# A hybrid SSD and attention layer: first pair's k copied by two engines, last product's matmuls pinned and cut, its stores on two queues

## The chip, the core and the metric

The kernel runs on one core of one Trainium2 chip. The metric is the device time of one execution in microseconds (us); the figure to be predicted is the median over repeated executions. Before the change it is 835.93 us, the median of three runs (835.86, 835.93 and 838.29).

The core's engines are TensorE (PE, with its weight loads as PEld), VectorE (DVE), ScalarE (ACT), GpSimd (POOL) and SyncE (SP), which here only issues DMAs.

## What is computed

One decoder layer over 512 tokens of width 1024. One projection of the normalised input feeds an SSD head group and a forgetting-attention head group of 16 heads of 64; then come an output projection, and a gated MLP of width 2816 with a short convolution. Cut to the two places that the change touches:

```python
qh = rms_norm(heads(q), q_norm_w)
kh = rms_norm(heads(k), k_norm_w)
for start in range(0, s, Q_BLOCK):                       # 128 queries at a time
    end = start + Q_BLOCK
    logits = einsum('bhqd,bhkd->bhqk', qh[:, :, start:end], kh[:, :, :end]) * scale
    logits = logits + cum[:, :, start:end, None] - cum[:, :, None, :end]
    p = softmax(where(causal, logits, -inf))
    outs.append(einsum('bhqk,bhkd->bhqd', p, vh[:, :, :end]))
...
h = causal_depthwise_conv(x @ w_up, conv_w, conv_b)
gate, val = split(h, 2, axis=-1)
x = x + (silu(gate) * val) @ w_down                      # 512 x 2816 times 2816 x 1024
```

## The kernel before

**Precision.** A float32 operand is split into a high part in float32r and a low part (the rest). `mm3` (L108 to L112) makes one product as three matmuls: high by high (L110), high by low (L111), low by high (L112). Weights are split as they arrive, by `load_split` (L99): SP loads `wraw`, ACT casts it to `wh` (L104), and DVE or POOL subtracts to make `wl` (L105).

**Order.** The program is recorded in source order, and a scheduler that models the engines then places the instructions of each engine's queue. `urgent()` (L594) raises the priority of what is recorded inside it, so attention work is slotted between projection matmuls. A changed dependency can therefore move many instructions in a stretch, not only the edited ones. Each queue executes in the order that it was given.

**Attention.** Heads are taken in pairs. `fox_qk` (L489) transposes a pair's normalised k and q into one PSUM bank each (`qkT`, L496). For k it writes head by head the high part (ACT, L503) and the low part (DVE, L504), each on that head's own 64 partitions, and then SP copies high and low together to the other 64 partitions with a DMA within SBUF (L506, 256 KB a head, 16 of them in the program). For q the high part goes to the own half and the low part to the other half. With k in both halves, one matmul over 128 partitions adds q high and q low. `fox_probs` (L510) then makes, for each of four query blocks, the scores `S` with two matmuls (k high L539, k low L540), the row maximum on DVE (L541), the exponential on ACT (L545), and after all four the reciprocal (L546) and the scaling (L549) on DVE. The biases `bias` (L524 to L529) are made ahead on ACT, DVE and POOL. `fox_values` (L552) transposes the probabilities (L566), splits them (L568, L569) and multiplies by v (L580).

While heads run, the projections of the next group of four heads serve as filler on PE: `token_block` (L318) with its matmuls into `pq`. After a block of q or k, ACT copies and squares it (L460, L462), DVE reduces (L463), POOL takes the power -1/2 (L122), and DVE scales `tok` (L468), which the next transposes (L496) need. v takes one ACT (L478) and one DVE instruction (L479) for each block.

**Last product.** The down projection is made of seven products of half size (`PRODUCTS`, L822). A product takes 11 blocks of 128 rows of its weight, in units of two (the last unit has one), for two token blocks `i`, each into its own PSUM bank. In the seventh (`Y`, lhs S3) the matmuls of the last two units are held and recorded together: 3 blocks x 2 token blocks x 3 matmuls = 18 matmuls of 512 columns, sorted by `i` (L865), though the scheduler is free to place them. When a bank is complete, DVE adds it to `x2` at column 0 and subtracts it at column 512 (L881), and SP stores the finished rows (L883); for `i` = 1 both are cut into halves of 256 columns. That makes six adds and six stores at the end of the program, all stores on SP's queue.

Of the kernel before, what the change touches and what calls it, by code (L numbers as in the profile page):

```python
# [10 lines left out]
AF = mybir.ActivationFunctionType  # L11
ALU = mybir.AluOpType
# [3 lines left out]
P = 128  # L16
# [39 lines left out]
def tile_hybrid_layer(  # L56
# [19 lines left out]
    nc = tc.nc  # L76
    act, dve, pool, pe = nc.scalar, nc.vector, nc.gpsimd, nc.tensor
# [10 lines left out]
    def raw(ap):  # L88
        return ap.bitcast(F32)
# [15 lines left out]
        (sub or dve).tensor_tensor(out=l, in0=r, in1=raw(h), op=ALU.subtract)  # L105
        return h, l

    def mm3(o, ah, al, bh, bl, start, stop, grouped=True):  # L108
        kw = {} if grouped else {"skip_group_check": True}
        pe.matmul(o, ah, bh, start=start, stop=False, **kw)  # L110
        pe.matmul(o, ah, bl, start=False, stop=False, **kw)  # L111
        pe.matmul(o, al, bh, start=False, stop=stop, **kw)  # L112

    def bank(name="g"):
        return pg.tile([P, 512], F32, tag="g", name=name)
# [373 lines left out]
    def fox_qk(pair, tq, tk):  # L489
        qs = [pf.tile([P, SEQ], F32R, tag="qs", name="qs", bufs=4) for _ in range(2)]  # L490
        ks = [pf.tile([P, 2, SEQ], F32R, tag="ks", name="ks", bufs=4) for _ in range(2)]
        pr = pair % 2
        for tok, w in ((tk, kw), (tq, qw8)):
            t = mbank("qkT")
            for tb in range(NTB):
                pe.transpose(t[:, tb * P : (tb + 1) * P], tok[:, tb, pr * P : (pr + 1) * P], ident)  # L496
            for hd, (own, other) in enumerate(HALVES):
                src, sw = t[own, :], w[own]
                if tok is tq:
                    h, l = qs[hd][own, :], qs[hd][other, :]  # L500
                else:
                    h, l = ks[hd][own, 0, :], ks[hd][own, 1, :]
                act.activation(h, src, AF.Copy, scale=sw)  # L503
                dve.scalar_tensor_tensor(out=l, in0=src, scalar=sw, in1=raw(h), op0=ALU.mult, op1=ALU.subtract)  # L504
                if tok is tk:
                    nc.sync.dma_start(raw(ks[hd][other, :, :]), raw(ks[hd][own, :, :]))  # L506
        osum = pf.tile([P, SEQ], F32, tag="osum", name="osum", bufs=2)
        return qs, ks, osum
# [334 lines left out]
    for n, (quarter, _, tiles, start, adds) in enumerate(PRODUCTS):  # L843
# [7 lines left out]
        for u, (lo, hi) in enumerate(UNITS):  # L851
# [9 lines left out]
                continue  # L861
            todo = [(k, i, b) for b in held for k in range(b[0], b[1]) for i in range(2)]
            held = []
            if final and u == len(UNITS) - 1:
                todo.sort(key=lambda t: t[1])  # L865
            for k, i, (lo_, _, h_, l_) in todo:
                c = slice((k - lo_) * 512, (k - lo_ + 1) * 512)
                s = slice(i * P, (i + 1) * P)
                mm3(
                    tiles[i], lhs[0][:, k, s], lhs[1][:, k, s], h_[:, c], l_[:, c], start and k == 0, k == NH - 1,  # L870
                    grouped=False,
                )
                if k == NH - 1:
                    for row, col, op, done in adds:
                        tb = row + i
                        cuts = 2 if final and i == 1 else 1
                        w = 512 // cuts
                        for cut in range(cuts):
                            c = slice(cut * w, (cut + 1) * w)
                            oc = slice(col + cut * w, col + (cut + 1) * w)  # L880
                            dve.tensor_tensor(out=x2[:, tb, oc], in0=x2[:, tb, oc], in1=tiles[i][:, c], op=op)  # L881
                            if done:
                                nc.sync.dma_start(out[tb * P : (tb + 1) * P, oc], x2[:, tb, oc])  # L883


def _feature(w, np):
# [74 lines left out]
```

## Time and profile before

| | |
|---|---|
| median of 3 runs | 835.93 us (835.86 to 838.29) |
| the profiled execution | 839.82 us, its span 838.0 us |
| busy share of the span | PE 97%, PEld 84%, DVE 75%, ACT 52%, POOL 35% |
| granted TensorE clock, mean | 0.995 |
| DMA | 98.76 MB, mean 118 GB/s |

The span runs from the first to the last instruction of the profiled execution; 1.8 us of its time lie outside. All positions below are microseconds from the start of that span. A busy PE in these tables includes the modelled end of pipelined matmuls, so the distance between the starts of two matmuls, not the duration shown, is what one costs in a stream.

### The profile page before, as it was taken

The page shows a single profiled execution, that of the slowest core. Times are in us where ns is not written, and L with a number is a line of the kernel's source. Part 1 is how long each engine was busy: PE and PEld are TensorE (multiplying, and loading weights), DVE is VectorE, ACT ScalarE, POOL GpSimd, SP SyncE. Part 2 cuts the span into 40 slices and gives each one's busy share as a digit, 9 for nine tenths or more (in the row PEclk, how much of TensorE's full clock was granted, in tenths as well). Part 3 has the DMA queues.
Part 4 walks back from the last instruction along what each step waited for, and adds up shares of the span by engine and source line. Part 5 has one row for each costly group of instructions (what it writes and reads, how often), then busy time and mean ns, then how long its engine had stood idle before and what let it go on. Part 6 is the DMA issues. An engine that isn't in the chain of part 4 may idle for free.

```text
span 838.0 us, 12428 instructions
## 1 busy us (share of the span) xinstructions
PE 810.0 (97%) x4590; PEld 700.4 (84%) x4590; DVE 630.9 (75%) x1015; ACT 435.9 (52%) x845; POOL 290.5 (35%) x281
## 2 busy tenths in 40 slices
PE   8999989899979999899999999999999999999997
PEld 5788879779979899799898898888888888888885
DVE  7596898775759798898999667666666666887744
ACT  5346645434456687576566255444433444656531
POOL 4125253365535445125233423333333332133120
PEclk9999999999989999999999999999999999999999
DMA  8424332341333333243422244233233223399992
GB/s 315 158 83 131 101 94 85 104 136 51 113 102 106 100 100 112 84 120 101 126 72 66 90 121 134 100 98 101 101 101 99 82 96 101 115 253 182 208 190 84
DMA packets 31565, 98.76 MB, mean 118 GB/s; under 512 B 4048, under 2 KB 5136, under 8 KB 31504
## 3 DMA queue, kind: packets, MB, share of 16 engines
q1 hardware_dynamic: 28048, 86.43, 31.9%
q0 software_dynamic: 3456, 11.54, 7.6%
q8 instruction: 36, 0.59, 0.3%
q14 instruction: 25, 0.20, 0.1%
HBM read 91.56 MB, written 2.20 MB: 112 GB/s over the span
## 4 chain that ended last, share of the span: by engine, by line
PE 73%; DVE 11%; issue 6%; POOL 3%; ACT 3%; DMA 2%; SPq 0%; DVEq 0%; POOLq 0%; ACTq 0%
PE up L112 10%; PE up L111 9%; PE up L110 9%; PE pq L111 4%; PE pq L112 4%; PE pq L110 4%; PE po L112 3%; PE po L111 3%; PE po L110 3%; DVE xs L351 2%; PE Y L110 2%; PE Y L112 2%; PE Y L111 2%; PE o L580 2%; PE pT L566 1%
## 5 line engine op out<-in xcount | busy, mean ns | idle before, releaser
L104 ACT CAST wh<-wraw 128x1024 fp32r<-128x1024 f32 x103 | 108.5, 1053 | 137.6 <-PE up L111 72.1
L110 PE MATMUL pq<-wh,xh 128*128 128x256 f32 x512 | 146.7, 289 | 0.0
L112 PE MATMUL pq<-wh,xl 128*128 128x256 f32 x512 | 146.7, 287 | 0.0
L111 PE MATMUL pq<-wl,xh 128*128 128x256 f32 x512 | 145.6, 285 | 0.5 <-DVE wl L105 0.5
L112 PE MATMUL up<-hh,wl 128*128 128x512 f32 (+1 forms) x368 | 140.2, 381 | 0.2 <-DVE wl L105 0.2
L111 PE MATMUL up<-hl,wh 128*128 128x512 f32 (+1 forms) x368 | 139.9, 380 | 0.0
L110 PE MATMUL up<-hh,wh 128*128 128x512 f32 (+1 forms) x368 | 139.8, 380 | 0.0
L105 POOL TENSOR_TENSOR wl<-wraw,wh 128x1024 fp32r<-128x1024 f32 x31 | 75.1, 2424 | 108.9 <-ACT wh L104 99.9
L105 DVE TENSOR_TENSOR wl<-wraw,wh 128x1024 fp32r<-128x1024 f32 x72 | 89.5, 1243 | 20.0 <-ACT wh L104 19.9
L111 PEld LDWEIGHTS pq<-wl,xh 128*128 128x128 f32 x512 | 98.2, 192 | 1.9 <-DVE wl L105 0.9
L110 PEld LDWEIGHTS pq<-wh,xh 128*128 128x128 f32 x512 | 98.0, 192 | 1.9 <-issue 1.2
L112 PEld LDWEIGHTS pq<-wh,xl 128*128 128x128 f32 x512 | 98.2, 192 | 0.7 <-issue 0.5
L112 PEld LDWEIGHTS up<-hh,wl 128*128 128x128 f32 x368 | 69.2, 188 | 13.5 <-DVE wl L105 0.4
L110 PEld LDWEIGHTS up<-hh,wh 128*128 128x128 f32 x368 | 69.1, 188 | 13.3 <-issue 0.2
L111 PEld LDWEIGHTS up<-hl,wh 128*128 128x128 f32 x368 | 69.2, 188 | 13.2
L773 DVE TENSOR_TENSOR up<-up,R 128x512 f32<-128x512 f32 x44 | 30.3, 691 | 57.0 <-PE up L112 57.0
L778 DVE SCALAR_TENSOR_TENSOR ua<-up,pc,ua 128x511 f32<-128x511 f32 (+1 forms) x88 | 67.2, 766 | 3.2 <-ACT ua L776 1.7
L526 POOL TENSOR_SCALAR bias<-cum,tokS 128x256 f32<-128x256 f32 (+1 forms) x32 | 22.5, 711 | 91.2 <-DVE nm L541 91.2
L545 ACT ACTIVATE prob<-prob,nm 128x128 f32<-128x128 f32 (+1 forms) x64 | 35.9, 562 | 29.6 <-DVE nm L541 29.3
L254 DVE TENSOR_TENSOR x<-po,x 128x512 f32<-128x512 f32 x64 | 43.3, 684 | 10.1 <-PE po L112 9.5
L734 ACT CAST wh<-T 128x1024 fp32r<-128x1024 f32 (+1 forms) x30 | 29.3, 978 | 37.5 <-PE Z L112 15.6
L735 DVE TENSOR_TENSOR wl<-T,wh 128x1024 fp32r<-128x1024 f32 (+1 forms) x30 | 33.8, 1133 | 19.7 <-ACT wh L734 19.7
(237 smaller groups left out, 1862.9 us busy)
## 6 DMA issues: line engine op xcount, KB each, us to landing
wraw<-in_wup_dram SPq DMA_DIRECT2D x44, 512.0 KB, 3.3
wraw<-in_wqkv_dram SPq DMA_DIRECT2D x24, 512.0 KB, 3.3
T<-in_wdown_dram POOLq DMA_DIRECT2D x20, 512.0 KB, 7.8
wraw<-in_wout_dram SPq DMA_DIRECT2D x16, 512.0 KB, 3.3
wraw<-in_wxbc_dram SPq DMA_DIRECT2D x11, 512.0 KB, 4.6
T<-in_wdown_dram SPq DMA_DIRECT2D x10, 512.0 KB, 5.1
wraw<-in_wdown_dram SPq DMA_DIRECT2D x10, 512.0 KB, 3.7
wraw<-in_wz_dram SPq DMA_DIRECT2D x8, 512.0 KB, 3.3
```

What stands on the lines that cost most here:

```text
L104: act.copy(h, r)
L105: (sub or dve).tensor_tensor(out=l, in0=r, in1=raw(h), op=ALU.subtract)
L110: pe.matmul(o, ah, bh, start=start, stop=False, **kw)
L111: pe.matmul(o, ah, bl, start=False, stop=False, **kw)
L112: pe.matmul(o, al, bh, start=False, stop=stop, **kw)
L254: dve.tensor_add(dst, o, dst)
L526: (dve if qb == 2 else pool).tensor_scalar(out=b, in0=cum[:, :n], scalar1=-1.0, scalar2=edge, op0=ALU.mult, op1=ALU.add)
L545: act.activation(p, p, AF.Exp, scale=-1.0, bias=nm[:, qb : qb + 1], accum_out=sm[:, qb : qb + 1])
L734: act.copy(h[:, :n], src[:, :n])
L735: dve.tensor_tensor(out=l[:, :n], in0=src[:, :n], in1=raw(h[:, :n]), op=ALU.subtract)
L773: dve.tensor_mul(xp, o, R2)
L778: dve.scalar_tensor_tensor(out=a[:, s:], in0=xp[:, : SEQ - s], scalar=pc[:, cw + 2 - s : cw + 3 - s], in1=a[:, s:], op0=ALU.mult, op1=ALU.add,
```

## The change

- In `fox_qk`, for the first pair of heads alone, the copy of k into the other 64 partitions is no longer a DMA. ACT writes the high part a second time from the same PSUM bank, and DVE the low part: two ACT and two DVE instructions of 64x512 more, two DMAs of 256 KB less. The other seven pairs keep the DMA.
- In the last two units of the last product, the matmuls keep the order of the program (`keep_in_program_order`): first the nine of token block 0 with 512 columns, then nine on columns 0 to 255 of token block 1, then nine on columns 256 to 511: 27 matmuls where there were 18.
- The adds are recorded behind them, token block 0 first, then the halves of token block 1. Of the six final stores, the three of columns from 512 on go to ACT's queue, the others stay with SP.

The diff, with the parts left out that only rename:

```diff
-    def mm3(o, ah, al, bh, bl, start, stop, grouped=True):
+    def mm3(o, ah, al, bh, bl, start, stop, grouped=True, keep=False):
         kw = {} if grouped else {"skip_group_check": True}
-        pe.matmul(o, ah, bh, start=start, stop=False, **kw)
-        pe.matmul(o, ah, bl, start=False, stop=False, **kw)
-        pe.matmul(o, al, bh, start=False, stop=stop, **kw)
+        for n, (a, b) in enumerate(((ah, bh), (ah, bl), (al, bh))):
+            ins = pe.matmul(o, a, b, start=start and n == 0, stop=stop and n == 2, **kw)
+            if keep:
+                tc.keep_in_program_order(ins)
...
                 dve.scalar_tensor_tensor(out=l, in0=src, scalar=sw, in1=raw(h), op0=ALU.mult, op1=ALU.subtract)
-                if tok is tk:
+                if tok is tk and pair == 0:
+                    act.activation(ks[hd][other, 0, :], src, AF.Copy, scale=sw)
+                    dve.scalar_tensor_tensor(
+                        out=ks[hd][other, 1, :], in0=src, scalar=sw, in1=raw(h), op0=ALU.mult, op1=ALU.subtract
+                    )
+                elif tok is tk:
                     nc.sync.dma_start(raw(ks[hd][other, :, :]), raw(ks[hd][own, :, :]))
...
+            def add_out(i, part_):
+                for row, col, op, done in adds:
+                    tb = row + i
+                    oc = slice(col + part_.start, col + part_.stop)
+                    dve.tensor_tensor(out=x2[:, tb, oc], in0=x2[:, tb, oc], in1=tiles[i][:, part_], op=op)
+                    if done:
+                        (nc.scalar if final and col else nc.sync).dma_start(
+                            out[tb * P : (tb + 1) * P, oc], x2[:, tb, oc]
+                        )
...
             if final and u == len(UNITS) - 1:
-                todo.sort(key=lambda t: t[1])
+                halves = (slice(0, 256), slice(256, 512))
+                for k, i, blk in todo:
+                    if i == 0:
+                        product(k, i, blk, whole, keep=True)
+                for half in halves:
+                    for k, i, blk in todo:
+                        if i == 1:
+                            product(k, i, blk, half, keep=True)
+                add_out(0, whole)
+                for half in halves:
+                    add_out(1, half)
+                continue
```

`product` calls `mm3` for one block of weight rows and the given columns of the bank.

The scheduler's order changes in two stretches alone: around the first heads of attention, and at the end.

**PE at the first head.** The names are `S` for scores (L539, L540, in the change L545, L546: k high, k low) and `pq` for projection filler (`mm3`, in the change all on L111). Before:

```order
L112 MATMUL pq<-wh,xl 128x256
L539 MATMUL S<-ks,qs 128x128
L540 MATMUL S<-ks,qs 128x128
L539 MATMUL S<-ks,qs 128x256
L540 MATMUL S<-ks,qs 128x256
L539 MATMUL S<-ks,qs 128x384
L540 MATMUL S<-ks,qs 128x384
L539 MATMUL S<-ks,qs 128x512
L540 MATMUL S<-ks,qs 128x512
L110 MATMUL pq<-wh,xh 128x256 x2
```

Now:

```order
L545 MATMUL S<-ks,qs 128x128
L545 MATMUL S<-ks,qs 128x256
L111 MATMUL pq<-wh,xl 128x256
L111 MATMUL pq<-wh,xh 128x256
L111 MATMUL pq<-wl,xh 128x256
L111 MATMUL pq<-wh,xl 128x256
L546 MATMUL S<-ks,qs 128x128
L546 MATMUL S<-ks,qs 128x256
L545 MATMUL S<-ks,qs 128x384
L546 MATMUL S<-ks,qs 128x384
L111 MATMUL pq<-wh,xh 128x256 x2
L111 MATMUL pq<-wl,xh 128x256
```

The first scores stand four filler matmuls earlier, they are no longer in one run, and the scores of the last query block (128x512) follow 23 filler matmuls behind those of the third.

**DVE at the same place.** `ks`, `qs` and `v` are the low parts of k, q and v; `prob,nm` is the row maximum of a score block. Before:

```order
L504 SCALAR_TENSOR_TENSOR ks<-qkT,pc,ks 64x512
L504 SCALAR_TENSOR_TENSOR qs<-qkT,qw_221,qs 64x512
L479 SCALAR_TENSOR_TENSOR v<-pq,r,v 128x2x64
L504 SCALAR_TENSOR_TENSOR ks<-qkT,pc,ks 64x512
L504 SCALAR_TENSOR_TENSOR qs<-qkT,qw_221,qs 64x512
L479 SCALAR_TENSOR_TENSOR v<-pq,r,v 128x2x64 x3
L541 ISA prob,nm<-S,bias 128x128
```

Now:

```order
L505 SCALAR_TENSOR_TENSOR ks<-qkT,pc,ks 64x512
L505 SCALAR_TENSOR_TENSOR qs<-qkT,qw_221,qs 64x512
L480 SCALAR_TENSOR_TENSOR v<-pq,r,v 128x2x64
L508 SCALAR_TENSOR_TENSOR ks<-qkT,pc,ks 64x512
L505 SCALAR_TENSOR_TENSOR qs<-qkT,qw_221,qs 64x512
L480 SCALAR_TENSOR_TENSOR v<-pq,r,v 128x2x64 x2
L505 SCALAR_TENSOR_TENSOR ks<-qkT,pc,ks 64x512
L547 ISA prob,nm<-S,bias 128x128
```

The second copy of the first head's k takes the place that the second head's k had; the second head's k follows two v instructions later, and its own second copy (L508) stands behind the first head's third score block. On ACT the same happens with L507.

**PE at the end.** `Y` are the two banks of the last product; `oh`, `ol` the high and low part of S3. The last rows before:

```order
L110 MATMUL Y<-wh,oh 128x512 x2
L111 MATMUL Y<-wl,oh 128x512
L112 MATMUL Y<-wh,ol 128x512
L110 MATMUL Y<-wh,oh 128x512
L111 MATMUL Y<-wl,oh 128x512
L112 MATMUL Y<-wh,ol 128x512
L111 MATMUL Y<-wl,oh 128x512
L112 MATMUL Y<-wh,ol 128x512
```

Now (the three rows of 128x512 come three times in a row, those of 128x256 six times, for three blocks and two halves):

```order
L111 MATMUL Y<-wh,oh 128x512
L111 MATMUL Y<-wl,oh 128x512
L111 MATMUL Y<-wh,ol 128x512
L111 MATMUL Y<-wh,oh 128x256
L111 MATMUL Y<-wl,oh 128x256
L111 MATMUL Y<-wh,ol 128x256
```

Before, the two banks were interleaved block by block to the end; now bank 0 is complete 18 half-width matmuls before the end, and the first half of bank 1 nine before it.

## Rows read from the trace of the kernel before

**Rows 1.** The page, its first part: busy time, share of the span, instructions.

```profile
PE 810.0 (97%) x4590; PEld 700.4 (84%) x4590; DVE 630.9 (75%) x1015; ACT 435.9 (52%) x845; POOL 290.5 (35%) x281
```

**Rows 2.** Windows: stretch, length, each engine's busy time, granted clock, DMA share, GB/s.

```profile
236.00:246.00 10.00, 5.88 (x27) 5.72 (x28) 3.11 (x12) 3.01 (x10) 3.13 (x7) 0.66 0.23 70
246.00:256.00 10.00, 10.00 (x83) 9.87 (x83) 8.49 (x21) 8.46 (x20) 5.06 (x7) 1.00 0.31 108
...
239.00:240.00 1.00, 0.00 (x0) 0.00 (x0) 0.00 (x0) 0.00 (x0) 0.00 (x0) 0.50 0.67 262
...
700.00:800.00 100.00, 100.00 (x440) 82.22 (x439) 76.45 (x94) 55.69 (x80) 25.25 (x26) 1.00 0.73 181
```

**Rows 3.** PE's waits from 225 to 300: in total, times, longest.

```profile
PE S L539 <- DMA ks<-ks: 4.5, 1, 4.5
PE qkT L496 <- DVE tok L468: 1.2, 1, 1.2
```

**Rows 4.** PE's timeline: start, duration, instruction, [idle before and its releaser].

```profile
231.11 0.28 PE L110 MATMUL pq<-wh,xh 128*128 128x256 f32 x1
231.23 0.28 PE L111 MATMUL pq<-wl,xh 128*128 128x256 f32 x1
...
235.31 0.28 PE L112 MATMUL pq<-wh,xl 128*128 128x256 f32 x1
240.12 0.45 PE L539 MATMUL S<-ks,qs 128*128 128x128 f32 x1 [4.53 <-DMA ks<-ks]
...
243.46 0.41 PE L110 MATMUL pq<-wh,xh 128*128 128x256 f32 x1
243.67 0.41 PE L111 MATMUL pq<-wl,xh 128*128 128x256 f32 x1
...
245.38 0.31 PE L110 MATMUL pq<-wh,xh 128*128 128x256 f32 x1
```

**Rows 5.** All 16 copies of k by DMA (L506): issue to landing.

```profile
DMA to landing us min/median/max: 2.8/2.9/8.3
```

**Rows 6.** ACT's and DVE's timelines from 231 to 251.

```profile
231.70 0.68 ACT L503 ACTIVATE ks<-qkT,pc 64x512 fp32r<-64x512 f32 x1
...
232.82 0.76 DVE L504 SCALAR_TENSOR_TENSOR ks<-qkT,pc,ks 64x512 fp32r<-64x512 f32 x1
...
240.94 0.29 DVE L541 CUSTOM_DVE_ANT_0 prob<-S,bias 128x128 f32<-128x128 f32 x1 [5.41 <-PE S L540]
...
241.81 0.42 DVE L541 CUSTOM_DVE_ANT_0 prob<-S,bias 128x256 f32<-128x256 f32 x1 [0.58 <-PE S L540]
...
246.13 0.29 DVE L541 CUSTOM_DVE_ANT_0 prob<-S,bias 128x128 f32<-128x128 f32 x1 [1.42 <-PE S L540]
...
250.75 0.18 DVE L546 RECIPROCAL sm<-sm 128x4 f32<-128x4 f32 x1 [1.24 <-ACT prob L545]
```

**Rows 7.** DVE's timeline: the two scalings of group 1's `tok`.

```profile
264.00 1.23 DVE L468 TENSOR_TENSOR tok<-tok,ms 128x1024 f32<-128x1024 f32 x1 [1.32 <-POOL ms L122]
...
282.63 3.42 DVE L468 TENSOR_TENSOR tok<-tok,ms 128x1024 f32<-128x1024 f32 x1 [2.80 <-POOL ms L122]
```

**Rows 8.** Timeline of the end, PE, DVE and SP.

```profile
831.58 0.39 PE L111 MATMUL Y<-wl,oh 128*128 128x512 f32 x1
...
831.78 2.61 DVE L881 TENSOR_TENSOR x<-x,Y 128x512 f32<-128x512 f32 x6 [5.08 <-PE Y L112]
831.81 0.40 PE L112 MATMUL Y<-wh,ol 128*128 128x512 f32 x1
...
833.98 0.41 DVE L881 TENSOR_TENSOR x<-x,Y 128x256 f32<-128x256 f32 x1
...
835.02 0.40 SPq L883 DMA_DIRECT2D out_dram<-x  x1
```

**Rows 9.** DMA issues: the last store of 835.02, and POOL's loads from 790 on.

```profile
out_dram<-x SPq DMA_DIRECT2D x1, 128.0 KB, 2.0
...
T<-in_wdown_dram POOLq DMA_DIRECT2D x5, 512.0 KB, 6.5
```

More of the change, by code (lines that the diff above doesn't have):

```diff
@@ L863, in tile_hybrid_layer, with product @@
             held = []
-            if final and u == len(UNITS) - 1:
-                todo.sort(key=lambda t: t[1])
[L866 to L872, printed above, removed]
-                if k == NH - 1:
[L874 to L883, printed above, removed]
+            def product(k, i, b, part_, keep=False):
+                lo_, _, h_, l_ = b
+                s = slice(i * P, (i + 1) * P)
+                c = slice((k - lo_) * 512 + part_.start, (k - lo_) * 512 + part_.stop)
+                mm3(
+                    tiles[i][:, part_], lhs[0][:, k, s], lhs[1][:, k, s], h_[:, c], l_[:, c], start and k == 0,
+                    k == NH - 1, grouped=False, keep=keep,
+                )
@@ new lines, in add_out @@
+            def add_out(i, part_):
[6 more added lines that the diff above has]
+                            out[tb * P : (tb + 1) * P, oc], x2[:, tb, oc]
+                        )
@@ new lines, in tile_hybrid_layer @@
+            whole = slice(0, 512)
+            if final and u == len(UNITS) - 1:
+                halves = (slice(0, 256), slice(256, 512))
[10 more added lines that the diff above has]
+                continue
@@ L886, in _feature @@
+            for k, i, blk in todo:
+                product(k, i, blk, whole)
+                if k == NH - 1:
+                    add_out(i, whole)
 def _feature(w, np):
```

## The prediction

> **What bounds the kernel now.** I read the page first: PE is busy for 97% of the span, DVE for 75%, the others for less [rows 1]. So time is won where PE stands still or runs slowly, or after its last matmul, and nowhere else. The windows then show where it stands still: from 236 to 246 PE is busy for 5.88 of 10 us and its granted clock averages 0.66, and in that stretch DVE, ACT and POOL are each busy for only about 3 [rows 2]. In the next ten PE is full at clock 1.00, and so it is in a hundred microseconds near the end (700 to 800) [rows 2]; what is won at 240 is therefore not soaked up by slack that late. The waits name the cause: the scores of the first head wait 4.5 us for the copy of k by DMA. From 225 to 300 the only other wait of PE over 1 us is one of 1.2 for `tok` [rows 3].
>
> PE's timeline shows what the wait costs behind it. The last filler starts at 235.31; the next matmul starts at 240.12, after 4.53 idle [rows 4]. By 239 the granted clock stood at 0.50, that is at 1.2 instead of 2.4 GHz [rows 2]. Filler matmuls that were 0.12 apart before the gap (231.11, 231.23) are 0.21 apart behind it (243.46, 243.67), until about 245.38 [rows 4]. The copy is an odd one: the median of all 16 copies lands 2.9 us after its issue, the slowest 8.3 [rows 5].
>
> The end of the program is the other place. The last matmul starts at 831.81 and takes 0.40, so PE ends at 832.21. DVE had waited 5.08 for a complete bank, and all six adds run from 831.78 on, the last from 833.98 to 834.39. SP's last store is issued at 835.02, 0.63 behind the add that it carries away [rows 8], and lands 2.0 later, at 837.02 [rows 9]; the span ends at 838.0.
>
> **The change at the first head.** Removed: two DMAs of 256 KB and the wait. The scores now need the second copy of the first head's k. It takes the place in ACT's and DVE's order that the second head's k had: ACT from 231.70 for 0.68, DVE from 232.82 for 0.76 [rows 6], so both parts lie there by 233.6. PE reaches the scores, now four fillers earlier, at 235.31 - 3 x 0.12 = 234.95 [rows 4]. The wait goes entirely.
>
> What that is worth for PE: 4.53 of idle time, and the slow stretch. From 240.12 to 245.38 are 5.26 us; at 0.12 for 0.21 this work takes 3.0 (2.26 less), at half the clock exactly 2.63 less. I take 2.4, since this stretch holds both filler and scores. Upper end for PE: 4.53 + 2.4 = 6.9.
>
> Added: one ACT and one DVE instruction for each of two heads, 2 x 0.68 and 2 x 0.76 [rows 6]. They lie in the time in which both engines now wait for the first scores. DVE is the tighter of the two, and it decides how much of PE's lead lasts, because the probabilities go through it. Up to the second head's reciprocal it idles 5.41 + 0.58 + 1.42 + 1.24 = 8.65 us [rows 6]. If all of this went and 1.5 of new work came, DVE would be 7.1 ahead, more than PE. If the last two waits stay (the second head's scores and ACT's exponential still follow each other in the new order), it is 7.1 - 1.42 - 1.24 = 4.5 ahead. So this part is worth between 4.5 and 6.9. I take **6.0**, nearer the upper end: in the new order 23 fillers stand between the third and fourth score blocks, so PE has other work while DVE catches up. If that cover were gone, PE would wait for DVE and the 4.5 would hold. Next in line is the second head's second copy, queued on DVE behind three row maxima of the first head, and then the 1.2 for `tok`, which I leave as it is.
>
> On SP the two copies leave the queue, and the loads behind them move up. I cost this at nothing: no wait for a weight load shows beside the copy [rows 3].
>
> **The change at the end.** PE: nine 512-wide matmuls 0.23 apart (831.58, 831.81) become eighteen 256-wide ones at 0.12 (the filler's width and distance) [rows 4, 8]: 2.07 becomes 2.16, 0.1 more, so PE ends at 832.3. In exchange bank 0 is complete 18 x 0.12 = 2.2 before the end and the first half of bank 1 is complete 1.1 before it. Four of the six adds fit beside these matmuls, for the six take 2.61 in all [rows 8]. Behind the last matmul only two 256-wide adds remain, at most 2 x 0.41 = 0.8 [rows 8], to 833.1. The store of the second goes to ACT's queue, on which only two earlier ones stand, and nothing follows. Issued at 833.1 instead of 835.02, it ends the program **1.9** earlier. What waits on SP now (a store every half microsecond behind its add) is split in two.
>
> The trace has no DMA issued by ACT. The nearest row, same tile and size from SP, lands in 2.0; the dearest other queue, POOL's loads of 512 KB, takes 6.5 [rows 9]. At 6.5 the end would come at 839.6 instead of 837.0, 2.6 later than now. I take 2.0, for it is the same store, and keep the other end for the range.
>
> **Sum.** 6.0 + 1.9 = 7.9. The profiled execution took 839.82 us, so it would take 831.9. It lies 3.9 above the median of the runs, 835.93. I carry the whole sum over: **828.0 us**.
>
> **Rival 1: the timed runs stall less than the profiled one.** The slow copy may be the profiled execution's own: other copies land in 2.9 [rows 5], and the execution is 3.9 longer than the median. If all 3.9 were this stall, the median becomes 831.9. If only the clock part were missing, the sum is 6.0 - 2.4 + 1.9 = 5.5, hence 830.4; the three runs, 838.29 against 835.9 twice, differ by about these 2.4. Against it: a profile lengthens other things too, and the copy stands behind the same loads in every run.
>
> The Trainium skill ("TensorE: Matmul & The Clock Gate", section "What's actually happening") says that the clock's change comes at a different point of the work from run to run; by that rule some runs of this kernel stall without the slow stretch, the 830.4 above. One trace cannot show it.
>
> **Rival 2: the lead is lost again.** PE waits for `tok` and its fellows anyway, and those chains of ACT, DVE and POOL may come no earlier. Then only the end is won: 834.0. For it speaks DVE at 8.49 of 10 us behind the stall [rows 2]; against it, that these chains begin with matmuls that come earlier.
>
> **Rival 3, slower: the lead becomes one new gap.** Its place is group 1's `tok`, which the transposes of the third pair need. If POOL's power and DVE's scaling come no earlier than now, PE stands there with its whole lead, 6.9 + 1.2 us, the clock falls as it did by 239, and the slow stretch costs 2.4 again: 835.93 + 2.4 - 1.9 = 836.4. If the first `tok` then also takes 3.42 instead of 1.23, as the second does [rows 7], it is 838.6. It decides as soon as `tok` gains less than about 3 us. For it: DVE waits for POOL there, 1.32 and 2.80 [rows 7].
>
> **Rival 4: ACT's stores are dear.** At POOL's 6.5 the end loses 4.5 against my sum: 832.5.
>
> **Numbers.** Forecast 48%, rival 1 28%, rival 2 11%, rival 3 7%, rival 4 6%. A measurement of this kernel tells 0.3%, 2.5 us, from no change: faster is below 833.4, slower above 838.4. Faster takes in the forecast and rivals 1 and 4: 82%. Rival 2 and half of rival 3 fall within: 14%. Slower: 4%. The range begins at 826.0: 6.9 + 1.9, and the wait of 1.2 for `tok` gone as well, are 10.0 less. It ends at 832.6, with rivals 1 and 4; rivals 2 and 3, 18%, lie outside.
>
> **What would show it.** In the new profile no wait of PE for `ks` at the first head; PE full and at clock 1.00 from 236 to 246; the first score about 235 instead of 240.1; the filler behind it 0.12 apart. At the end: four adds before the last matmul, two behind it; ACT's last store issued 0.8 behind PE's end, landing in about 2. Wrong would be a new gap of PE before 300, above all at a transpose for `tok` or a score block behind DVE; a landing of ACT's store far above 2; or a median that falls by 2 to 4 although the profile shows all of this, which is rival 1.

## The result, and the profile after

The changed kernel takes 828.99 us, the median of four runs (828.33 to 830.26), beside 836.89 for the kernel before on the same chip (835.86 to 838.29): a ratio of 0.9906, 95% interval 0.9884 to 0.9929. That is 7.9 us less. Its profiled execution took 829.39 us with a span of 827.6; the spans of the two profiled executions differ by 10.4, more than the medians do. That gap between 7.9 and 10.4 has to be explained too. One execution of head_only (its profiled one) and one of before_low_dve (both kernels are described below) took 2062 and 1620 us and stand in no median below, so head_only has no profile to read.

The page's first part, and the windows of the changed kernel (as [rows 1, 2]):

```profile
PE 807.4 (98%) x4599; PEld 698.7 (84%) x4599; DVE 629.7 (76%) x1017; ACT 437.2 (53%) x847; POOL 293.8 (36%) x281
```

```profile
236.00:246.00 10.00, 10.00 (x83) 9.82 (x81) 8.78 (x28) 8.02 (x24) 5.88 (x8) 1.00 0.33 97
246.00:256.00 10.00, 10.00 (x84) 9.91 (x83) 9.71 (x23) 7.81 (x17) 5.61 (x7) 1.00 0.48 131
276.00:286.00 10.00, 10.00 (x84) 9.91 (x84) 7.44 (x18) 7.95 (x19) 2.83 (x2) 1.00 0.46 117
...
326.00:336.00 10.00, 7.50 (x55) 6.53 (x54) 7.14 (x10) 4.75 (x11) 3.70 (x2) 1.00 0.18 60
```

From 236 to 246 PE is busy for all of 10.00 us where it was for 5.88, and the granted clock is 1.00 instead of 0.66. What is left stands later: 2.5 us are missing from 326 to 336.

PE's timeline at the first head (as [rows 4]):

```profile
234.80 0.39 PE L545 MATMUL S<-ks,qs 128*128 128x128 f32 x2
235.03 0.28 PE L111 MATMUL pq<-wh,xl 128*128 128x256 f32 x1
...
235.50 0.40 PE L546 MATMUL S<-ks,qs 128*128 128x128 f32 x2
...
236.32 0.28 PE L111 MATMUL pq<-wl,xh 128*128 128x256 f32 x1
236.44 0.28 PE L111 MATMUL pq<-wh,xl 128*128 128x256 f32 x1
```

The first score starts at 234.80 instead of 240.12, without a wait, and the filler behind it goes at 0.12.

PE's waits from 225 to 350, before (more of the view of [rows 3], which ended at 300):

```profile
PE S L539 <- DMA ks<-ks: 4.9, 2, 4.5
PE qkT L496 <- DVE tok L468: 2.5, 2, 1.3
PE po L110 <- DVE v L479: 1.2, 1, 1.2
PE pT L566 <- DVE nm L541: 0.6, 1, 0.6
PE pq L111 <- DVE wl L105: 0.5, 1, 0.5
```

and in the changed kernel, from 225 to 345:

```profile
PE qkT L497 <- DVE tok L469: 1.3, 1, 1.3
PE po L111 <- DVE v L480: 1.2, 1, 1.2
PE pT L572 <- DVE nm L547: 0.7, 1, 0.7
```

`po` is the output projection's product and `pT` the transposed probabilities. The waits for `ks` are gone. So are two that the change doesn't touch: 1.17 for group 1's second `tok`, and 0.46 for a `wl` ahead of it. Three of before's remain, all of group 2: 1.3 for `tok`, 1.2 for `v` and 0.7 for `nm`.

The end, on DVE, SP and ACT (as [rows 8]):

```profile
820.80 1.28 DVE L884 TENSOR_TENSOR x<-x,Y 128x512 f32<-128x512 f32 x2 [3.49 <-PE Y L111]
822.93 1.41 DVE L884 TENSOR_TENSOR x<-x,Y 128x256 f32<-128x256 f32 x4 [0.86 <-PE Y L111]
...
821.51 2.86 SPq L886 DMA_DIRECT2D out_dram<-x  x3
...
L886 ACTq DMA_DIRECT2D out_dram<-x x3: 338/339/383, 822.1 to 824.4; - x3
...
DMA to landing us min/median/max: 1.8/2.0/2.1
```

PE's last matmul starts at 822.62 and ends at 822.90. The last row is the landing of these six stores. Only two adds stand beside matmuls. All four of token block 1 start behind the very last one, the two of the first half too, whose columns were complete 1.1 us before. ACT's last store is issued 1.5 us behind PE's end; before, SP's last was 2.8 behind it.

**One way to divide the span.** The transposes of k and q (`qkT`) begin the attention and end with the last pair, so their first and last start cut the span in three: what lies ahead, the attention, and the rest with the MLP and the end. In this table the last column but one sums the gaps between one matmul's end and the next one's start, inside the middle stretch, from PE's timeline.

| profiled execution | first `qkT` | first to last | PE idle in it | last `qkT` to the end |
|---|---|---|---|---|
| before | 229.5 | 199.9 | 9.7 | 408.7 |
| before_again (below) | 228.8 | 198.3 | 8.7 | 408.6 |
| changed | 229.4 | 190.6 | 3.3 | 407.6 |
| tail_only | 228.1 | 196.0 | 8.0 | 407.5 |
| head_act_queue | 229.5 | 191.5 | 3.2 | 407.4 |
| head_double | 228.6 | 187.6 | 0.8 | 407.6 |
| all_pairs | 230.4 | 188.2 | 0.5 | 407.6 |
| v2_low_dve | 228.9 | 186.3 | 0.1 | 407.5 |
| before_low_dve | 228.6 | 191.5 | 4.7 | 408.7 |
| tail_whole | 228.8 | 190.7 | 3.5 | 407.5 |
| tail_one_queue | 229.0 | 191.0 | 3.8 | 407.9 |
| tail_bank | 230.3 | 190.6 | 3.5 | 407.3 |
| best | 231.2 | 186.5 | 0.1 | 407.3 |

The first column varies by 3 us between executions, whatever the change; the last falls into groups by the end that a kernel has: 408.6 to 408.7 for the old one, 407.3 to 407.9 for the new one and its variants. The change is worth 1.0 to 1.1 in the last column and 7.7 to 9.3 in the middle.

### The profile page after: what moved, and what is told of

The parts are those of the page before. It is cut to its first block, busy times and chain, and to the rows that moved or that the text cites. A ratio compares the mean times of both kernels' runs of the same rounds, so it can differ in the third digit from the quotient of the medians.

```text
span 827.6 us, 12438 instructions
## 1 busy us (share of the span) xinstructions
PE 807.4 (98%) x4599; PEld 698.7 (84%) x4599; DVE 629.7 (76%) x1017; ACT 437.2 (53%) x847; POOL 293.8 (36%) x281
## 4 chain that ended last, share of the span: by engine, by line
PE 80%; DVE 10%; issue 3%; ACT 3%; DMA 2%; POOL 1%; SPq 0%; DVEq 0%; POOLq 0%; ACTq 0%
PE up L111 29%; PE pq L111 16%; PE po L111 10%; PE Y L111 5%; PE Z L111 4%; PE X L111 4%; DVE xs L352 2%; PE g L111 2%; PE o L586 2%; PE pT L572 2%; DMA sc<-cs_d 1%; PE yd L416 1%; PE S L546 1%; PE S L545 1%; DVE wl L105 1%
## 5 line engine op out<-in xcount | busy, mean ns | idle before, releaser
L111 PE MATMUL pq<-wh,xl 128*128 128x256 f32 x512 | 146.3, 286 | 0.0
L111 PE MATMUL pq<-wh,xh 128*128 128x256 f32 x512 | 146.0, 287 | 0.0
L111 PE MATMUL pq<-wl,xh 128*128 128x256 f32 x512 | 145.1, 284 | 0.0
L111 PE MATMUL up<-hh,wl 128*128 128x512 f32 (+1 forms) x368 | 140.2, 381 | 0.2 <-DVE wl L105 0.2
L111 PE MATMUL up<-hl,wh 128*128 128x512 f32 (+1 forms) x368 | 139.9, 380 | 0.0
L111 PE MATMUL up<-hh,wh 128*128 128x512 f32 (+1 forms) x368 | 139.8, 380 | 0.0
L111 PEld LDWEIGHTS pq<-wl,xh 128*128 128x128 f32 x512 | 97.6, 191 | 1.3 <-issue 0.5
L111 PEld LDWEIGHTS pq<-wh,xh 128*128 128x128 f32 x512 | 97.2, 191 | 1.8 <-issue 1.2
L111 PEld LDWEIGHTS pq<-wh,xl 128*128 128x128 f32 x512 | 97.6, 191 | 0.7 <-issue 0.5
L111 PEld LDWEIGHTS up<-hh,wl 128*128 128x128 f32 x368 | 69.2, 188 | 13.8 <-DVE wl L105 0.4
L111 PEld LDWEIGHTS up<-hh,wh 128*128 128x128 f32 x368 | 69.1, 188 | 13.2 <-issue 0.2
L111 PEld LDWEIGHTS up<-hl,wh 128*128 128x128 f32 x368 | 69.2, 188 | 13.0
L794 POOL TENSOR_TENSOR ua<-ua 128x512 f32<-128x512 f32 x11 | 15.0, 1365 | 93.7 <-DVE ua L784 93.7
```

The source lines that it names most:

```text
L111: ins = pe.matmul(o, a, b, start=start and n == 0, stop=stop and n == 2, **kw)
```

## The experiments

Times of all of them; each ratio is to the kernel before in the same job.

| kernel | median, us (runs, range) | ratio, 95% interval |
|---|---|---|
| head_only | 830.03 (3, 829.49 to 830.65) | 0.991, 0.9893 to 0.9928 |
| tail_only | 836.52 (12, 833.34 to 839.21) | 0.9991, 0.9974 to 1.0007 |
| head_act_queue | 829.80 (4, 828.54 to 830.43) | 0.9905, 0.989 to 0.9921 |
| head_double | 826.12 (4, 825.53 to 826.87) | 0.9864, 0.9848 to 0.9879 |
| tail_bank | 829.82 (6, 827.79 to 830.41) | 0.9904, 0.988 to 0.9927 |
| tail_whole | 829.58 (5, 828.76 to 830.01) | 0.9906, 0.9883 to 0.9928 |
| v2_low_dve | 824.47 (4, 823.96 to 825.94) | 0.9849, 0.9824 to 0.9875 |
| all_pairs | 826.34 (5, 824.83 to 828.01) | 0.9869, 0.9846 to 0.9893 |
| before_again | 837.46 (1) | |
| before_low_dve | 833.01 (11, 830.57 to 835.83) | 0.9952, 0.9934 to 0.9971 |
| tail_one_queue | 829.30 (6, 828.54 to 830.17) | 0.991, 0.9892 to 0.9927 |
| best | 824.97 (5, 822.97 to 826.69) | 0.9853, 0.9829 to 0.9876 |

In these jobs the kernel before ran 17, 11 and 16 times: medians 837.35, 837.84 and 837.35, from 833.4 to 841.1. Its 44 runs spread over 7.7 us, which is itself a finding; the changed kernel's four lie within 1.9.

### The two parts apart: head_only and tail_only

`head_only` is the kernel before with the new branch in `fox_qk`; `tail_only` is the changed kernel with the old one:

```diff
-                if tok is tk and pair == 0:
-                    act.activation(ks[hd][other, 0, :], src, AF.Copy, scale=sw)
-                    dve.scalar_tensor_tensor(
-                        out=ks[hd][other, 1, :], in0=src, scalar=sw, in1=raw(h), op0=ALU.mult, op1=ALU.subtract
-                    )
-                elif tok is tk:
+                if tok is tk:
```

> The duplication of the first pair's k alone, the end as before. Theory: the whole stall was the late copy, and the lead it gives is kept to the end. Then no wait of PE between 225 and 300 us is over 1.5 us, the granted clock from 236 to 246 is 1.00, the time from the last but one unit on is as before, and the median falls by 7.9 less what the end is worth (1.0 in the traces): 6.9 us, to about 830.0. Rival: the timed runs stall less than the profiled one and part of the gain of the median comes from the end: then the median falls by under 6, while this kernel's profiled span is still some 9.4 shorter (828.6).

> The new end alone, the first head as before. Theory: all four adds of the second token block wait for the last matmul, so the end gains 1.0 to 1.3 us, not 1.9: median about 835.8, and the time from the end of PE to the end of the span is 4.7 as in the changed kernel. Rival: the end gains the 1.9 of the prediction, or more (median 835.0 or less). Its profile is a second look at the unchanged first head: if the stall of 4.5 us and the clock of 0.66 from 236 to 246 stand there again, they are the kernel's and not one execution's.

Measured: the head alone 830.03, as expected (a ratio of 0.991, that is 7.5 us); the end alone 0.9991, 0.8 us with an interval from a gain of 2.2 to a loss of 0.6. Its profile tells it more closely: 407.5 in the last column beside 408.6 to 408.7, a gain of 1.1. The head is what the change is about, and the end gains 1.0 to 1.1 instead of 1.9.

The second profile of the unchanged first head is not what the first was. Of `tail_only`, PE's timeline, the window, and the two copies' landing:

```profile
236.89 0.30 PE L540 MATMUL S<-ks,qs 128*128 128x128 f32 x1 [2.72 <-DMA ks<-ks]
```

```profile
236.00:246.00 10.00, 9.11 (x72) 8.97 (x73) 7.19 (x27) 7.33 (x22) 4.57 (x9) 1.00 0.27 82
```

```profile
DMA to landing us min/median/max: 5.3/5.9/6.5
```

A stall of 2.72 us, not 4.53; the copy landed in 6.5 instead of 8.3; and the clock did not fall at all. This execution took 833.34, the shortest of its twelve.

### A second profile of the kernel before: before_again

The kernel before, unchanged.

> The kernel before once more, for a second profile. Theory: the stall at the first head stands in every run, but its length follows the copy's landing: between 2.7 us (profile of the new end alone) and 4.5 (first profile), and the clock falls only behind the longer ones; two or three scalings of tok take 3.4 and cost PE another 3 to 5 us. Rival: 4.5 and the low clock are the rule: then they stand here within 0.3 us.

PE's timeline, the window, and the landing:

```profile
238.66 0.30 PE L539 MATMUL S<-ks,qs 128*128 128x128 f32 x1 [3.77 <-DMA ks<-ks]
```

```profile
236.00:246.00 10.00, 7.34 (x43) 7.09 (x44) 5.25 (x21) 4.05 (x14) 2.46 (x7) 0.83 0.29 89
```

```profile
DMA to landing us min/median/max: 6.5/7.1/7.6
```

The theory holds here: 3.77 us of stall, clock 0.83. The executions of the unchanged head with a profile now make a series: landing 8.3, 7.6, 6.5 and 6.2 us (the last is before_low_dve, below), stall 4.53, 3.77, 2.72 and 2.39. The landing less the stall is 3.8 in all four. So the landing sets the stall, and it varies by 2 us between these four executions of the same copy.

The slow clock can be sized the same way. Stretch less idle time is 190.2 in the first profile, 189.6 in the second, and 188.0 in `tail_only`, whose clock stayed at 1.00 and whose order in this stretch is the same: the slow clock cost 2.2 us in the first and 1.6 in the second. This execution took 837.46, right at the kernel's median.

### The copy by DMA from another queue: head_act_queue

```diff
-                if tok is tk and pair == 0:
...
-                elif tok is tk:
-                    nc.sync.dma_start(raw(ks[hd][other, :, :]), raw(ks[hd][own, :, :]))
+                if tok is tk:
+                    (nc.scalar if pair == 0 else nc.sync).dma_start(raw(ks[hd][other, :, :]), raw(ks[hd][own, :, :]))
```

> The changed kernel, but the first pair's k is copied by DMA as before, issued by ScalarE on its own empty queue instead of SyncE's. Theory: the copy of 8.3 us was late because of what stood before it and beside it in the DMA engines, not because of the queue that issued it: it lands some 5 to 8 us after its issue, PE waits 2 to 4.5 us, the clock falls, and the time is 832 to 837. Rival: SyncE's queue itself made it late: then it lands in 2 to 3, PE waits under 1, and the time is within 1.5 us of the changed kernel's 829.

The longest wait, the window, and the landing:

```profile
PE S L540 <- DMA ks<-ks: 3.2, 3, 2.5
```

```profile
236.00:246.00 10.00, 7.99 (x49) 7.73 (x50) 5.61 (x22) 4.92 (x15) 3.44 (x7) 0.83 0.32 100
```

```profile
DMA to landing us min/median/max: 5.1/5.7/6.3
```

The copy is not late because of SP's queue: from a queue with nothing ahead of it, it still takes 6.3. What is left of the theory's causes is the other transfers in the DMA engines, whose share was 1.02 from 234 to 236; no run varies that load, so this part is not shown. PE stalls 2.5 and the clock falls to 0.83, although it stayed at 1.00 behind the 2.72 of `tail_only`. But the time is 829.8, within 1 us of the kernel without any stall, where the theory wanted 832 to 837. A stall that costs nothing is a contradiction until one looks further down: this kernel has no wait at all between 260 and 345, where the changed one has 1.3, 1.2 and 0.7. It lost at 236 and won at 330. Something else decides several microseconds there; what it is comes out below, at the collision.

### What the added work costs: head_double and all_pairs

`head_double` writes the duplicates twice:

```diff
+                    for _ in range(2):
-                    act.activation(ks[hd][other, 0, :], src, AF.Copy, scale=sw)
-                    dve.scalar_tensor_tensor(
+                        act.activation(ks[hd][other, 0, :], src, AF.Copy, scale=sw)
+                        dve.scalar_tensor_tensor(
...
```

`all_pairs` drops the condition on the pair:

```diff
-                if tok is tk and pair == 0:
+                if tok is tk:
...
-                elif tok is tk:
-                    nc.sync.dma_start(raw(ks[hd][other, :, :]), raw(ks[hd][own, :, :]))
```

> The changed kernel with each of the duplicates written twice: 1.5 us more of VectorE's and 1.4 us more of ScalarE's time, in the same stretch as the change's own work. Theory: this work lies where both engines were idle and costs nothing: within 0.5 us of the changed kernel's 829.0, and PE without a wait over 1 us from 225 to 260. Rival: VectorE sets the lead, as the sum of the prediction had it for its lower bound: then the time is 1.4 to 2.0 longer, 830.4 to 831.

> The changed kernel with all eight pairs' k duplicated by ScalarE and VectorE, no DMA. Theory: the other fourteen copies land before they are needed (median 2.9 us), so nothing is won there, and 14 x 0.76 = 10.6 us more of VectorE's time, in a stretch where it is busy for over 8 of 10 us, costs some of it: 830 to 836. Rival: the added work hides everywhere as it does at the first pair, or copies still held up the scores here and there: 827 to 829.5.

Both missed, on the good side: 826.1 and 826.3, both about 3 us below the changed kernel, with more work on DVE. So VectorE does not set the lead at the first head, and even 14 more of its 0.76 us can be hidden. What makes them faster shows in the waits: in both, those around 330 are gone (PE idle 0.8 and 0.5 us in the middle stretch, beside 3.3). The order had moved there too: POOL has a mask instruction (`bias`) between its power on `ms` and the subtraction for `wl`, which in the changed kernel follow one another directly.

### The collision: v2_low_dve and before_low_dve

What the order moves can be read from POOL beside DVE. The kernel before, timelines of POOL and DVE from 262 to 290 (the scaling at 282.63 is in [rows 7]):

```profile
278.76 3.84 POOL L122 TENSOR_TENSOR ms<-ms,mhalf 128x16 f32<-128x16 f32 x1 [2.42 <-DVE ms L121]
282.58 2.40 POOL L105 TENSOR_TENSOR wl<-wraw,wh 128x1024 fp32r<-128x1024 f32 x1
```

and the changed kernel, DVE and POOL:

```profile
272.95 1.23 DVE L469 TENSOR_TENSOR tok<-tok,ms 128x1024 f32<-128x1024 f32 x1 [0.96 <-POOL ms L123]
...
270.00 2.91 POOL L123 TENSOR_TENSOR ms<-ms,mhalf 128x16 f32<-128x16 f32 x1 [1.55 <-DVE ms L122]
273.10 3.34 POOL L105 TENSOR_TENSOR wl<-wraw,wh 128x1024 fp32r<-128x1024 f32 x1 [0.18 <-ACT wh L104]
...
327.37 3.41 DVE L469 TENSOR_TENSOR tok<-tok,ms 128x1024 f32<-128x1024 f32 x1 [1.85 <-POOL ms L123]
...
327.30 2.40 POOL L105 TENSOR_TENSOR wl<-wraw,wh 128x1024 fp32r<-128x1024 f32 x1
```

POOL's power on `ms` releases DVE's scaling of `tok`. If a subtraction for a weight's low part stands next on POOL, it starts at once, 0.05 us before the scaling, and the scaling takes 3.42 instead of 1.23: POOL is done at 284.98, and DVE 1.07 behind it, at 286.05: nearly its whole undisturbed 1.23. In the changed kernel that subtraction waited 0.18 us for ACT, the scaling came first with 1.23, and POOL paid instead, 3.34 for 2.40. The Trainium skill ("SBUF — State Buffer", section "Who interferes with whom") says that a DVE instruction with two SBUF inputs contends with a GpSimd instruction that reads SBUF, and that issue order decides who blocks. For this pair the rows agree: 3.42 for 1.23 where POOL was first, 3.34 for 2.40 where DVE was. Two more offsets fit: in the changed kernel the scalings at 210.6 and 392.3, which begin 0.45 and 1.18 us after such a subtraction, take 3.02 and 2.30, and like the others they end 1.07 to 1.09 behind it. In that kernel the pair also collides at 309.3 and 327.4, 3.41 each.

To test it, one letter of the table that says who computes a weight's low part:

```diff
-    "v2": "pd",
+    "v2": "dd",
```

in the changed kernel; in `before_low_dve`, the same for `v1` and `v2` in the kernel before.

> The changed kernel, but the low part of the third group's first v weight is computed by VectorE instead of GpSimd. Theory: in the changed kernel VectorE's scaling of tok at 327.4 takes 3.41 instead of 1.23 because GpSimd began this subtraction 0.07 before it, and the two cannot run side by side; PE then waits 1.32 for tok and 1.18 behind it. Without the subtraction on GpSimd the scaling takes 1.23, those two waits are gone or under 0.5 each, and the time is 1.3 to 2.5 shorter: 826.5 to 827.7. Rival: tok's scaling is slow by itself, or the 1.2 us more of VectorE's work cost as much: time within 0.7 of 829.0 or longer.

> The kernel before with one edit that has nothing to do with the change: the low part of the second and third group's first v weight goes from GpSimd to VectorE. Theory: that alone frees tok at 282.6 and 336.7 (3.4 to 1.25 us each) and with it PE's waits of 0.46, 1.17, 1.30 and 1.18 us: 3 to 5 us less, 832.5 to 834.5 with the first stall still there; so what the change gained beyond the stall itself was a shift of such collisions. Rival: behind the stall VectorE has no room and the 2.4 us more of its work cost as much: within 1.5 us of 837.

The first: 824.47, a gain of 4.5, more than expected. DVE's scalings and POOL in that kernel:

```profile
308.86 1.23 DVE L469 TENSOR_TENSOR tok<-tok,ms 128x1024 f32<-128x1024 f32 x1
...
323.36 1.30 DVE L469 TENSOR_TENSOR tok<-tok,ms 128x1024 f32<-128x1024 f32 x1 [1.30 <-POOL ms L123]
...
320.43 2.91 POOL L123 TENSOR_TENSOR ms<-ms,mhalf 128x16 f32<-128x16 f32 x1
323.30 2.02 POOL L535 TENSOR_SCALAR_AFFINE_SELECT bias<-bias 128x128 f32<-128x128 f32 x4
325.29 2.39 POOL L105 TENSOR_TENSOR wl<-wraw,wh 128x1024 fp32r<-128x1024 f32 x1
```

Both scalings are short. The edit took away the subtraction at 309, not the one expected; ahead of the other the scheduler now put four mask instructions of some 0.3 us each. The scaling had to wait for the first alone (323.30 + 0.3 + the same 1.07 is 324.67, and it ends at 324.66), and POOL paid, with 2.02 for the four where the changed kernel's four at 261.64 take 1.05. PE idles 0.1 us in the whole middle stretch, although a later scaling, at 386.1, now takes 3.42: no wait of PE stands behind that one. Of the 4.3 that the stretch is shorter, 3.2 are idle time; the other 1.1 I cannot assign.

The second: 833.0 and a ratio of 0.9952, a gain of 4.0 without the change, inside what the theory named. But the place is only half right. PE's waits from 225 to 345:

```profile
PE S L539 <- DMA ks<-ks: 3.4, 2, 2.4
PE qkT L496 <- DVE tok L468: 1.3, 1, 1.3
```

The scaling at 276.4 still collides (3.42, with another subtraction next on POOL), and so one wait for `tok` is left; the two of group 2 (1.22 each) do not, and group 2's waits for `tok`, `v` and `nm` are gone. A new one of 1.0 for `ks` stands at 336.9.

The other profiles bear the collision out. The second scaling of group 1 takes 3.41 to 3.42 in four of the thirteen executions (before, before_again, tail_only, before_low_dve), and in each PE waits 1.16 to 1.30 for it; in the other nine it takes 1.21 to 1.23, and PE does not wait. The second scaling of group 2 takes 3.41 in seven (before, before_again, tail_only, changed, tail_whole, tail_one_queue, tail_bank), each with a wait of 1.30 to 1.32 for it and one of 1.15 to 1.19 behind that; in the six others it takes 1.22 to 1.30, and no wait over 0.3 is left there. Those six include head_act_queue, head_double and all_pairs: this is what they won at 330. The first scaling of group 2 collides in these three as well (3.40 to 3.41), and PE does not wait for it.

One row goes the other way. In before_low_dve two `bias` instructions of POOL begin 0.24 us before the scaling, and still the scaling takes its undisturbed 1.22 and POOL pays, with 2.40 for the two where two of the same shapes take 1.25 at 274.10 in the kernel before:

```profile
326.08 2.40 POOL L526 TENSOR_SCALAR bias<-cum,tokS 128x256 f32<-128x256 f32 x2
...
326.32 1.22 DVE L468 TENSOR_TENSOR tok<-tok,ms 128x1024 f32<-128x1024 f32 x1
```

So the earlier start decides between the scaling and the subtraction, but not against every POOL instruction; why is open.

### The end, taken apart: tail_whole, tail_one_queue, tail_bank

`tail_whole` drops the halves from the matmuls, `tail_one_queue` the second queue, and `tail_bank` gives the second half of token block 1 its own PSUM bank for the last nine matmuls, with two more adds for what the old bank held:

```diff
-                for half in halves:
-                    for k, i, blk in todo:
-                        if i == 1:
-                            product(k, i, blk, half, keep=True)
+                for k, i, blk in todo:
+                    if i == 1:
+                        product(k, i, blk, whole, keep=True)
```

```diff
-                        (nc.scalar if final and col else nc.sync).dma_start(
+                        nc.sync.dma_start(
```

```diff
+                spare = po.tile([P, 512], F32, tag="o", name="spare")
...
+                for n, (k, i, blk) in enumerate(ones_):
+                    product(k, i, blk, halves[1], keep=True, dst=spare, first=n == 0)
+                add_out(1, halves[1], store=False)
                 add_out(0, whole)
+                add_out(1, halves[0])
+                add_out(1, halves[1], src=spare)
```

> The changed kernel, but the second token block's last products in whole 512-wide matmuls again; fixed order, adds in halves and two queues stay. Theory: the split of the matmuls gains nothing, since the adds wait for the bank anyway: the end is the changed kernel's within 0.15 us (4.7 from PE's end to the span's), the median within 0.5. Rival: the halves let adds start sooner: then this is 0.5 to 1.0 slower.

> The changed kernel with all stores of the end on SyncE's queue again; the fixed order stays. Theory: the fixed order, which puts the two adds of the first token block beside matmuls, and the second queue share the 1.0 us: SyncE's last issue stands 0.5 to 0.8 later, the time from the last transpose of k and q to the end of the span is 408.1 to 408.4 instead of 407.6. Rival A: the queue gives it all (408.6, as before). Rival B: the queue gives nothing (407.6).

> The changed kernel, but the last products of the second half of the second token block go into a PSUM bank of their own, with two more adds of 256 columns for what the old bank held. Theory: the adds wait for the whole bank, not for their columns. Then the first half's two adds start beside the last nine matmuls and only two adds stand behind PE's end: the time from PE's end to the end of the span falls from 4.7 to 4.0, the median by 0.7 to 828.3. Rival: the adds are held back by something else (VectorE's own order, the stores): all four stand behind PE's end still, and the time is the changed kernel's within 0.3.

Without the halves the end is as long (407.5 and 407.6 in the last column), and all four adds start behind the last matmul as before. So the split of the matmuls is worth nothing. On one queue it is 407.9: the second queue is worth 0.3 to 0.4, a little less than expected, and the fixed order the other 0.7. With a bank of its own, DVE's timeline, and PE's last matmul:

```profile
821.68 2.61 DVE L884 TENSOR_TENSOR x<-x,Y 128x512 f32<-128x512 f32 x6 [3.49 <-PE Y L111]
824.21 0.74 DVE L884 TENSOR_TENSOR x<-x,spare 128x256 f32<-128x256 f32 x2
```

```profile
823.50 0.28 PE L111 MATMUL spare<-wh,ol 128*128 128x256 f32 x1
```

Now six adds run without a break, five of them begun before PE's last matmul ends at 823.78. So what held the first half's adds was that both halves shared one tile in one bank; the edit separates tile and bank at once and does not show which of the two counts. The gain is 0.1 to 0.3 (407.3 beside 407.4 to 407.6), not the 0.7 expected: eight adds one after the other, from 821.68 to 824.95, now reach past PE's end at 823.78 by 1.2. DVE has become the bound there. The median, 829.82 with an interval of about 2 us either way, cannot show 0.3.

### Together: best

`tail_bank` with the edit of `v2_low_dve`: the `+` lines of `spare` above, and

```diff
-    "v2": "pd",
+    "v2": "dd",
```

> The changed kernel with the two edits that helped: the third group's first v weight's low part on VectorE, and a PSUM bank of its own for the last half of the end. Theory: they add: 824.5 less 0.3, that is 824.2, and no wait of PE between the first and the last transpose of k and q over 0.3 us. Rival: the end's separate bank is worth nothing in the median: 824.5 or a little over.

824.97 (822.97 to 826.69): not to be told from 824.47. The middle stretch (186.5) and the end (407.3) are as expected, but this execution began its attention 2 us later (231.2), in a part that the edits leave alone: from 164 to 168 its granted clock was 0.55, where the changed kernel's was 1.00. The version to keep is `v2_low_dve`, one letter from the changed kernel and 1.5% below the kernel before.

## Why the prediction came out right

The number was right, 828.0 forecast and 828.99 measured, and the likeliest case with it. Point by point it was less so: two terms were too large, a gain that the sum did not hold made up for them, and that the total lies within 1 us is in part luck.

- **The wait goes, PE stays full, the clock stays up**: as forecast, the first score at 234.80 (234.95 forecast), filler 0.12 apart.
- **What that is worth, between 4.5 and 6.9, 6.0 taken**: the lower bound supposed that DVE sets the lead. It does not: `head_double` puts 1.5 us more on DVE and loses nothing. PE's upper end was the right one for that execution: 4.53 of idle time and 2.2 of slow clock, where 2.4 was taken.
- **"The 1.2 for `tok`, which I leave as it is"**: it went, with 0.46 ahead of it. The key was in [rows 7]: one scaling of 1.23 and one of 3.42 with the same shape. I used the 3.42 for a rival and did not ask what made it. It was a collision with POOL, and a change of order can remove or make such a collision, for 1.2 us here; the 0.46 is a wait for a `wl` ahead of it and went with the order too.
- **The end, 1.9**: mis-sized; it measures 1.0 to 1.1. The step that failed is "four of the six adds fit beside these matmuls": the first half's adds wait for the last matmul of their bank, so four stand behind it, not two, and the last store is issued 1.5 behind PE's end, not 0.8. The stores on ACT's queue were as cheap as taken: the end's six stores land in 1.8 to 2.1.
- **"I carry the whole sum over"**: the profiled execution had the longest stall of the four with a profile, 4.53 beside 3.77, 2.72 and 2.39. Rival 1 was right in its mechanism. The span of before_again is 2.3 shorter than the first profile's: 1.0 is the shorter wait, 0.6 the shorter slow stretch, and 0.7 an earlier start of the attention. That is most of the gap between 10.4 and 7.9. The argument against this rival, that a profile lengthens other things, the runs do not bear out: the profiled execution of `tail_only` is the shortest of its twelve, and that of `v2_low_dve` lies at the median (824.51 and 824.47). The rule beside it, that the clock's change comes at a different point from run to run (the Trainium skill, "TensorE: Matmul & The Clock Gate", section "What's actually happening"), fits the rows: the same head ran at 0.66, 0.83 and twice at 1.00. But here the stalls differed too.

The books close on before_again, the execution at the median. Its middle stretch is 7.7 longer than the changed kernel's: 5.4 of idle time (3.77 at the first head, 1.6 at `tok` and `wl`), 1.6 of slow clock, and 0.7 not assigned. With 1.0 at the end that is 8.7, less 0.6 because it began its attention earlier: 8.1 between these two spans, where the medians differ by 7.9. Against the forecast of 7.9: the first head's 6.0 was in truth 5.4 in a typical run, the end 1.0 instead of 1.9, and 2.3 came from what the sum did not hold.

Rivals 2 and 3 fell: the lead is there at the end of the attention, and `tok` gained 7.0 and 9.7 us (264.00 to 256.95, 282.63 to 272.95; against before_again 4.7 and 7.4), well above the 3 below which rival 3 decides. Rival 4 fell with the landing.

## What to carry to other kernels

A profile is one execution: where the cause is a transfer that lands late, look at a second before pricing the stall, for its length varied almost by a factor of two here. When one line of the program has two durations for the same shape, find out why before forecasting anything behind it: here two engines held each other up, and one letter that kept such instructions apart was worth more (4.5 us) than the end's whole rewrite (1.1). And the adds here did not start on the finished half of a PSUM tile while matmuls still wrote the rest; with a bank of its own for the second half they did.

## What the runs showed of the hardware that I had not expected

- DVE's `tok` multiply (both inputs in SBUF) beside POOL's subtraction takes 3.41 us instead of 1.23, or makes POOL's take 3.34 instead of 2.40; of these two the one that starts earlier, by 0.05 to 0.15 us, keeps its full pace. A `tensor_scalar` of DVE suffers alike: in the kernel before, four scalings of probabilities that begin 0.36 us after such a subtraction take 3.32 instead of 1.45 (the first alone 2.22, until 0.09 after the subtraction's end at 270.84):

```profile
268.35 2.49 POOL L105 TENSOR_TENSOR wl<-wraw,wh 128x1024 fp32r<-128x1024 f32 x1
...
268.71 3.32 DVE L549 TENSOR_SCALAR prob<-prob,sm 128x128 f32<-128x128 f32 x4
...
275.76 1.45 DVE L549 TENSOR_SCALAR prob<-prob,sm 128x128 f32<-128x128 f32 x4
```

- The clock of 236 to 246 fell to 0.66 behind a stall of 4.53 us and to 0.83 behind 3.77, stayed at 1.00 behind 2.72 and 2.39, yet fell to 0.83 behind 2.5 in `head_act_queue`. The stall's length alone does not decide; why is open.
- Moving the copy to an empty queue did not make it faster (6.3 us, beside 6.2 to 8.3 from SP's). The median of all 16 copies, most of them later in the attention, is 2.9.
